# Moving the inverted 64-blocks of the second layer in transfers of sixteen partitions, from one spill tensor

## The chip, the cores and the metric

The kernel runs on one core of a Trainium2 chip. The metric is the time of one execution in device microseconds; the lower the better. TensorE (PE) does the matrix products, VectorE (DVE), ScalarE (ACT) and GpSimd (POOL) the elementwise work, and SyncE (SP) issues every DMA of this kernel, in the order of its program. An engine that waits holds up everything behind it in its own program.

## The reference, cut to what matters

The program is one step of a two-layer decoder for a prompt of 512 tokens and 8 samples. The change lies in the second layer, a gated DeltaNet with 16 query/key heads (the kernel calls each, with its two value heads, a pair) over 512 tokens. The prompt is cut into chunks; in each chunk and value head a unit lower triangular matrix is inverted and applied:

```
lmat = jnp.where(strict, jnp.einsum('bhnid,bhnjd->bhnij', kb, kc) * decay, 0.0)
tmat = lax.linalg.triangular_solve(lmat + eye, eye, left_side=True, lower=True, unit_diagonal=True)
u_val = tmat @ (vc * bc[..., None])
w_key = tmat @ (kb * jnp.exp(gc)[..., None])
...
v_new = u_n - w_n @ s
o_n = qd_n @ s + a_n @ v_new
s = s * gl_n[..., None, None] + jnp.swapaxes(kd_n, -1, -2) @ v_new
```

## The kernel before, in words

The weights are streamed: a half matrix of 512 KB (tile `wr`, three buffers) is loaded, split into a high part `wh` on ACT and a low part `wl` on DVE, and used by 48 matmuls of 260 columns into a `pg` tile. A `gemm` is two such halves.

Every call of an engine is recorded, and `flush` lays the instructions out with a planner: it keeps a clock for each engine, takes costs from the function `cost`, and writes each engine's instructions in the order of their planned start. For a DMA it plans an issue time on SP; a transfer over 20 KB that touches at most 8 partitions ("few", line 260) is planned at 1700 ns of SP, the others at 340 or 560 ns. Order is decided by these planned times; on the chip each engine follows the written order, whatever the times become. Each DMA also waits until the transfer eight issues before it has landed.

The second layer runs in two phases.

- **Phase one** (pool `l1a`). For each pair i, `prepare(i)` projects and convolves q and k (tiles `buf`, `cacc`, `kq`), forms the decay-weighted products and writes q, k, the product `it` and the lower triangular `lt` to `spill[i]` in DRAM: 4 chunks of 128 tokens x 128 partitions x 7 x 128 values, the slots 5 and 6 being `lt` of the two heads. After pair 15 come seven pairs of gate projections (`zd`, stored from tile `dd` with the DMA `z<-dd`).
- **Phase two** (pool `l1b`, which takes the memory of `l1a`). For each pair `values(i)` projects v (tiles `vc`, `vs`), `scan(i)` loads the four chunks of `spill[i]` (tile `pk`, four buffers) and runs the recurrence, `samples(i)` handles the 8 samples with the state tile `S`, and `normalise(i)` closes the pair.

`inverses(b8)` inverts the two 64x64 diagonal blocks of every chunk and head of eight pairs at once: 2 blocks x 8 pairs x 2 heads x 4 chunks are 128 matrices, one in each partition of tile `m` (128 x 64 x 64). It loads them from `spill`, works on DVE with some 120 products and reductions (`tmp<-m`, `m<-tmp`), and stores them back into `spill`. Loads and stores go block by block, pair by pair and head by head, four partitions each (one for each chunk): 32 transfers of 64 KB to load, 32 to store. Batch 0 (pairs 0 to 7) is recorded after pair 7 of phase one, with low urgency, batch 1 (pairs 8 to 15) in pieces over phase two (`background`). `scan(i)` needs the stores of its pair.

Of the kernel before, what the change touches and what calls it, by code (L numbers as in the profile page):

```python
# [8 lines left out]
F32 = mybir.dt.float32  # L9
# [6 lines left out]
P = 128  # L16
# [11 lines left out]
GQ = 16  # L28
# [10 lines left out]
class Sched:  # L39
# [79 lines left out]
    def region(self, ap):  # L119
        rec = self.owner.get(ap.tensor.name)  # L120
        if rec is None:
            return None
        dims, off = tuple(tuple(x) for x in ap.ap), ap.offset
        if ap.space == bass.MemoryType.DRAM:
            lo = off + sum(min(0, s * (c - 1)) for s, c in dims)
            hi = off + sum(max(0, s * (c - 1)) for s, c in dims)
            return rec, lo, hi + 1, 1
        if ap.space == bass.MemoryType.PSUM:
            return rec, 0, P, 1
        fs = 1  # L130
        for x in rec["shape"][1:]:
            fs *= x
        key = (off % fs, dims[1:])
        m = self.masks.get(key)
        if m is None:
            idx = np.array([off % fs])
            for s, c in dims[1:]:
                if s:
                    idx = (idx[:, None] + s * np.arange(c)[None, :]).reshape(-1)
            b = np.zeros(idx.max() + 1, np.uint8)  # L140
            b[idx] = 1
            m = self.masks[key] = int.from_bytes(np.packbits(b, bitorder="little").tobytes(), "little")
        p0 = off // fs
        return rec, p0, p0 + dims[0][1], m

    def record(self, eng, meth, fn, args, kw, out=None, ins=None, cost=None):
        isap = lambda x: isinstance(x, bass.AP)
# [81 lines left out]
    def cost(self, eng, meth, args, kw, out, ins):  # L229

        n = self.free(out)
        PSM = bass.MemoryType.PSUM
        big = [x for x in ins if not (self.free(x) == 1 and n > 1)]
        ptr = len(ins) - len(big)
        nps = sum(1 for x in ins if x.space == PSM)
        acc = kw.get("accum_out") is not None
        if eng == "PE":
            k, m = ins[0].shape[0], out.shape[0]
            rows = 32 if k <= 32 else 64 if k <= 64 else 128
            if meth == "transpose":  # L240
                return max(109 if rows == 128 else 82, 0.833 * n + 2), (rows, 128), "t"
            if ins[1].dtype == F32R:
                return (max(120, 0.417 * n + 6) if rows == 128 else 0.833 * n + 8), (rows, 128), "r"
            cols = 32 if m <= 32 else 64 if m <= 64 else 128
            if (rows, cols) == (128, 32):
                return max(100, 1.667 * n + 52), (rows, cols), "q"
            return 2 * max(109 if rows == 128 else 58, 0.833 * n + 3), (rows, cols), "f"
        if eng == "ACT":
            f = args[2] if meth == "activation" else AF.Copy
            return 0.83 * n + (58 if nps else 109) + 93 * ptr + 105 * acc, f  # L250
        if eng == "SP":
            by, run = int(4 * np.prod(out.shape)), 4096
            for x in [out] + ins:
                r = 1
                for st, c in reversed([tuple(d) for d in (x.ap if x.space == bass.MemoryType.DRAM else list(x.ap)[1:])]):
                    if st != r:
                        break
                    r *= c
                run = min(run, 4 * r)
            few = any(x.space != bass.MemoryType.DRAM and x.shape[0] <= 8 for x in [out] + ins) and by > 20000  # L260
            return (1700 if few else 340 if by / run <= 130 else 560), int(by * (1 + 77 / run if run >= 512 else 512 / max(run, 64)))
        two = sum(1 for x in big if x.space != PSM) > 1
        if eng == "DVE":
            fast = meth in ("tensor_scalar", "tensor_copy") and not nps and out.space != PSM
            if meth == "memset":
                return 0.52 * n + 60, True
            if meth == "reciprocal":
                return 6.6 * n + 70, False
            if meth == "tensor_tensor_scan":
                return 2.09 * n + 55, two  # L270
            if meth == "tensor_reduce":
                return 1.04 * self.free(ins[0]) + 65, False
            r = 0.52 if fast else 1.04
            if meth == "tensor_tensor" and n >= 100:
                inner = [[d for d in list(x.ap)[1:] if d[1] > 1] for x in big]
                if any(d and abs(d[-1][0]) > 4 for d in inner):
                    r = 1.83
            return r * n + 68 + 60 * ptr + 12 * acc, two or fast
        if meth == "tensor_tensor":
            return 1.57 * n + 430, True  # L280
        if meth == "tensor_reduce":
            return 2.1 * self.free(ins[0]) + 100, True
        if meth == "memset":
            return 0.5 * n + 130, True
        return 0.83 * n + 370 + 60 * ptr, True
# [198 lines left out]
def build(tc, a, ctx):  # L484
# [11 lines left out]
    dr = sc.pool(ctx, "dr", 1, DR)  # L496
# [610 lines left out]
    with ExitStack() as es:  # L1107
# [62 lines left out]
        for k in range(8):  # L1170
            for ip in range(len(X), max(k // 2 + 1, (k + 1) * KB // 8 // 2)):
                residual(ip)
            x = X[k // 2][:, k % 2]
# [46 lines left out]

    spill = [dr.tile([4, P, 7, P], F32, name=f"sp{i}") for i in range(GQ)]
    NZ = 7
    zd = [dr.tile([P, NT], F32, name=f"z{h}") for h in range(2 * GQ)]
    y1d = [dr.tile([P, NT], F32, name=f"y1_{h}") for h in range(NH)]
    with ExitStack() as l1:
# [124 lines left out]
        def inverses(b8, iv):  # L1352
            m = iv.tile([P, 64, 64], F32, name="m")
            blocks = []
            for blk in range(2):
                for i in range(8):
                    for hd in range(2):
                        p0 = blk * 64 + i * 8 + hd * 4
                        dv = spill[8 * b8 + i][:, blk * 64:blk * 64 + 64, 5 + hd, blk * 64:blk * 64 + 64]
                        blocks.append((m[p0:p0 + 4], dv))  # L1360
            for s, dv in blocks:
                Q.dma_start(s, dv)
            mf = m.rearrange("p j i -> p (j i)")
            V.memset(mf[:, 0::65], 1.0)
            pr = m[:, 32:64, 0:32]

            def dot(out, x, y):
                shape = x.shape[1:]
                n = int(np.prod(shape))
                tv = iv.tile([P, 1024], F32, name="tmp")[:, :n]  # L1370
                if len(shape) == 2:
                    tv = tv.rearrange("p (a b) -> p a b", a=shape[0])
                else:
                    tv = tv.rearrange("p (k a b) -> p k a b", k=shape[0], a=shape[1])
                V.tensor_tensor(tv, x, y, op=ALU.mult)
                V.tensor_reduce(out, tv, op=ALU.add, axis=AX.X)
                return n

            def diag(r0, nr, c0, nc_, step, nb):

                r = m[:, r0:r0 + nr, c0:c0 + nc_]
                return bass.AP(tensor=r.tensor, offset=r.offset, ap=[r.ap[0], [step * 65, nb], [64, nr], [1, nc_]])

            def over(x, n):

                return x.broadcast_to([P, x.shape[1], n, x.shape[3]])

            turn = lambda x: x.rearrange("p k a b -> p k b a")
            yield 0
            for i in range(1, 8):  # L1390
                x, col = diag(0, i, 0, i, 8, 8), diag(0, i, i, 1, 8, 8)
                yield dot(col[:, :, :, 0], x, over(turn(col), i))
            for s_ in (8, 16, 32):
                nb = 32 // s_
                prb = lambda j0, j1, k0, k1: bass.AP(tensor=pr.tensor, offset=pr.offset + 64 * j0 + k0,
                                                     ap=[pr.ap[0], [s_, nb], [64, j1 - j0], [1, k1 - k0]])
                for j in range(s_):
                    x = over(diag(j, 1, j, s_ - j, 2 * s_, nb), s_)
                    y = turn(diag(j, s_ - j, s_, s_, 2 * s_, nb))
                    yield dot(prb(j, j + 1, 0, s_)[:, :, 0, :], x, y)  # L1400
                for i in range(s_):
                    x = over(turn(diag(s_, i + 1, s_ + i, 1, 2 * s_, nb)), s_)
                    yield dot(diag(0, s_, s_ + i, 1, 2 * s_, nb)[:, :, :, 0], x, prb(0, s_, 0, i + 1))
            V.memset(pr, 0.0)
            for s, dv in blocks:
                Q.dma_start(dv, s)
# [69 lines left out]
        with ExitStack() as l1a:  # L1476
# [3 lines left out]
            for i in range(GQ):  # L1480
# [5 lines left out]
                if i in (1, 3, 5, 6)[:4 - 3]:  # L1486
                    ada(1, 8 + 3 + (1, 3, 5, 6).index(i), lk)
            back = [inverses(1, iv), 0]

            def background(n):  # L1490
# [273 lines left out]
        for i in range(GQ):  # L1764
# [4 lines left out]
            vs, dv = values(i)  # L1769
# [150 lines left out]
```

## Time and profile before

| | us |
|---|---|
| median of 3 runs | 3327.67 (3323.73 to 3341.83) |
| the profiled execution | 3313.89 |
| its span, first to last instruction | 3312.1 |
| PE busy in the span | 3108.7 (94%) |
| DVE busy | 2341.9 (71%) |
| ACT busy | 1566.5 (47%) |

Phase one of the second layer runs from about 1280 to 1870 us of the span, phase two to about 2920. A line of the trace gives the start, the duration, the engine, the operation, the tile written and the tiles read; what stands in brackets is the idle time of the engine before it, and what ended that. Since all instructions are laid out by one function, they carry the same line number (L418), and they are told apart by their tiles.

### The profile page before, as it was taken

The numbers are of one execution on the slowest core, as the hardware profiler recorded it, in microseconds if no ns is written. First come the engines' busy times: TensorE is split into PE (matmuls) and PEld (weight loads), VectorE is DVE, ScalarE is ACT, GpSimd is POOL, SyncE is SP. The second block draws the span as 40 slices with busy tenths as digits, with TensorE's granted clock in tenths as the row PEclk, the third lists the DMA queues.
The fourth block names the chain that finished last, engine by engine and source line by source line (L and its number), as shares of the span: only waits on it lengthen the run. The fifth ranks groups of instructions, "written<-read, shape, count | busy, mean of one in ns | idle before, by whom it ended". The sixth has DMA issues, their size and how long they took to land. (4 is left out here: it accounts for less than half of the span.)

```text
span 3312.1 us, 65624 instructions
## 1 busy us (share of the span) xinstructions
PE 3108.7 (94%) x24496; PEld 2806.7 (85%) x24496; DVE 2341.9 (71%) x6214; ACT 1566.5 (47%) x2927; POOL 342.6 (10%) x301
## 2 busy tenths in 40 slices
PE   8999999989979999999999668999989999999997
PEld 5898888877867777999999667987878989999997
DVE  3487989787864485668999426998975766566755
ACT  2234344434552366777652124545444655554544
POOL 0000000000001011111110011111112110101111
PEclk9999999999979999999999888998989999999999
DMA  9978989998538886776653255544446545376764
GB/s 317 298 256 290 316 299 315 304 319 305 175 119 282 296 294 210 162 163 151 146 151 116 74 113 145 140 141 145 139 126 186 149 145 161 119 231 211 225 185 139
DMA packets 361586, 667.02 MB, mean 201 GB/s; under 512 B 103697, under 2 KB 216338, under 8 KB 357170
## 3 DMA queue, kind: packets, MB, share of 16 engines
q1 hardware_dynamic: 361266, 662.82, 65.4%
q8 instruction: 193, 3.16, 0.4%
q14 instruction: 127, 1.04, 0.1%
HBM read 574.95 MB, written 87.70 MB: 200 GB/s over the span
## 5 line engine op out<-in xcount | busy, mean ns | idle before, releaser
L418 PE MATMUL pg<-uh,wh 128*128 128x260 f32 (+1 forms) x6112 | 1343.9, 289 | 6.6 <-ACT uh L418 3.1
L418 PE MATMUL pg<-ul,wh 128*128 128x260 f32 (+1 forms) x6112 | 1339.8, 289 | 1.5 <-DVE ul L418 1.1
L418 PEld LDWEIGHTS pg<-uh,wh 128*128 128x128 f32 (+1 forms) x6112 | 998.3, 190 | 62.2 <-issue 46.6
L418 PEld LDWEIGHTS pg<-ul,wh 128*128 128x128 f32 (+1 forms) x6112 | 998.9, 190 | 56.1 <-issue 43.6
L418 PE MATMUL pg<-uh,wl 128*128 128x260 f32 (+1 forms) x6112 | 892.0, 289 | 0.0
L418 DVE TENSOR_TENSOR wl<-wr,wh 128x1024 fp32r<-128x1024 f32 (+3 forms) x508 | 618.7, 1218 | 382.6 <-PE pg L418 161.5
L418 ACT CAST wh<-wr 128x1024 fp32r<-128x1024 f32 (+3 forms) x508 | 511.4, 1007 | 791.9 <-PE pg L418 671.3
L418 PEld LDWEIGHTS pg<-uh,wl 128*128 128x128 f32 (+1 forms) x6112 | 793.2, 190 | 46.6 <-issue 39.2
L418 DVE SCALAR_TENSOR_TENSOR junk<-page,qbc 128x128 f32<-128x128 f32 x1024 | 222.6, 284 | 9.7 <-ACT qbc L418 6.2
L418 DVE TENSOR_TENSOR tmp<-m 128x224 f32<-128x224 f32 (+19 forms) x238 | 214.5, 901 | 4.5
L418 DVE SCALAR_TENSOR_TENSOR acc<-gp,conv_w_a,acc 128x512 f32<-128x512 f32 x240 | 181.0, 754 | 6.6 <-ACT acc L418 3.9
L418 ACT ACT_TABLE_LOAD x120 | 154.0, 1283 | 49.8 <-DVE rs L418 19.5
L418 DVE TENSOR_REDUCE m<-tmp 128x32 f32<-128x224 f32 (+19 forms) x238 | 130.7, 549 | 3.3
L418 POOL TENSOR_SCALAR ctap<-buf,conv_w_c 128x512 f32<-128x512 f32 x64 | 72.7, 1135 | 524.9 <-ACT buf L418 521.5
L418 POOL TENSOR_TENSOR cacc<-cacc,ctap 128x512 f32<-128x512 f32 x64 | 84.9, 1326 | 388.6 <-DVE cacc L418 340.8
L418 DVE SCALAR_TENSOR_TENSOR cacc<-buf,conv_w_c,cacc 128x512 f32<-128x512 f32 x128 | 99.9, 781 | 13.9 <-ACT cacc L418 9.6
L418 PE MATMUL pl<-wa,cpad 128*32 128x512 f32 x512 | 81.0, 604 | 5.8 <-DMA wa<-w_ada 5.6
L418 DVE DVE_READ_ACCUMULATOR junk<-page,qbc 128x1 f32 x1024 | 81.4, 79 | 0.0
L418 PE MATMUL pg<-yh,wh 128*128 128x260 f32 x320 | 79.1, 283 | 0.0
L418 PE MATMUL pg<-yl,wh 128*128 128x260 f32 x320 | 78.9, 283 | 0.0
L418 POOL TENSOR_TENSOR S<-S,egb 128x2048 f32<-128x2048 f32 x16 | 59.5, 3722 | 165.4 <-PE pd L418 165.4
L418 PE MATMUL pl<-page,wst 128*32 128x512 f32 x512 | 75.1, 611 | 0.2
(377 smaller groups left out, 3615.5 us busy)
## 6 DMA issues: line engine op xcount, KB each, us to landing
wr<-w_in_odd SPq DMA_DIRECT2D x194, 512.0 KB
page<-cache_k SPq DMA_DIRECT2D x128, 512.0 KB
wa<-w_ada SPq DMA_DIRECT2D x128, 512.0 KB
page<-cache_v SPq DMA_DIRECT2D x128, 512.0 KB
wr<-w_out_odd SPq DMA_DIRECT2D x128, 512.0 KB
wr<-w_in_even SPq DMA_DIRECT2D x94, 512.0 KB
page<-w_ada SPq DMA_DIRECT2D x128, 256.0 KB
pk<-sp SPq DMA_DIRECT2D x64, 448.0 KB
```

What stands on the lines that cost most here:

```text
L418: o[2](*o[3], **o[4])
```

## The change

There is now one DRAM tensor `sp` for all pairs, 64 chunks x 128 x 7 x 128, of which `spill[i]` is a view. In `inverses` the partitions of `m` are dealt out anew: sixteen neighbouring partitions hold the four chunks of four neighbouring pairs for one block and one head, and they move in one transfer of 256 KB. There are 8 transfers instead of 32 to load a batch, and 8 instead of 32 to store it; the bytes and the length of the rows (64 values, 256 bytes) stay. The planner learns to tell the blocks of `sp` apart (`parts`), and prices transfers of up to 16 partitions as "few". What is computed is the same.

```
-            few = any(x.space != bass.MemoryType.DRAM and x.shape[0] <= 8 for x in [out] + ins) and by > 20000
+            few = any(x.space != bass.MemoryType.DRAM and x.shape[0] <= 16 for x in [out] + ins) and by > 20000
...
-    spill = [dr.tile([4, P, 7, P], F32, name=f"sp{i}") for i in range(GQ)]
+    spa = dr.tile([4 * GQ, P, 7, P], F32, name="sp")
+    spill = [spa[4 * i:4 * i + 4] for i in range(GQ)]
...
-            for blk in range(2):
-                for i in range(8):
+            for i in (0, 4):
+                for blk in range(2):
                     for hd in range(2):
-                        p0 = blk * 64 + i * 8 + hd * 4
-                        dv = spill[8 * b8 + i][:, blk * 64:blk * 64 + 64, 5 + hd, blk * 64:blk * 64 + 64]
-                        blocks.append((m[p0:p0 + 4], dv))
+                        p0 = 64 * blk + 32 * hd + 4 * i
+                        c0, r = 4 * (8 * b8 + i), slice(64 * blk, 64 * blk + 64)
+                        blocks.append((m[p0:p0 + 16], spa[c0:c0 + 16, r, 5 + hd, r]))
```

The planned order moves with it. On SP, at the end of phase one, the order before was this (the `z` stores are the last two gate stores, `wr` the weights of the second value head of pair 0):

```order
L418 DMA z_17871<-dd 128x520
L418 DMA wr<-w_in_odd 128x1024 x2
L418 DMA sp_17843<-m 4x64x64
...
L418 DMA sp_17850<-m 4x64x64
L418 DMA z_17872<-dd 128x520
L418 DMA sp_17850<-m 4x64x64
L418 DMA wr<-w_in_odd 128x1024
L418 DMA win<-state_conv_c 128x2x24
```

Now the same place reads:

```order
L431 DMA wr<-w_in_odd 128x1024 x2
L431 DMA sp<-m 16x64x64 x8
L431 DMA z_17856<-dd 128x520
L431 DMA z_17857<-dd 128x520
L431 DMA wr<-w_in_odd 128x1024 x3
L431 DMA win<-state_conv_c 128x2x24
L431 DMA zt<-z_17844 128x520
L431 DMA zt<-z_17845 128x520
L431 DMA pk<-sp 128x896 x3
```

Between the stores of the batch and the last gate store stood 31 transfers, now there are eight; but both last gate stores and the weights of pair 0's second value head now stand behind the stores, where one gate store and no such weight did.

On DVE, in phase one, the start of batch 0 (`MEMSET m`, which sets the diagonals) stood behind the work of pair 8:

```order
L418 SCALAR_TENSOR_TENSOR cacc<-buf,conv_w_c,cacc 128x512
L418 TENSOR_TENSOR wl<-wr,wh 128x1024
L418 TENSOR_TENSOR kql<-kq,kqh 128x1024
...
L418 TENSOR_TENSOR bet<-bet,ss 128x4x2
L418 MEMSET m 128x64
L418 TENSOR_SCALAR nb<-bet 128x8
```

Now it stands ahead of it:

```order
L431 SCALAR_TENSOR_TENSOR cacc<-buf,conv_w_c,cacc 128x512
L431 MEMSET m 128x64
L431 TENSOR_TENSOR tmp<-m 128x8
L431 TENSOR_REDUCE m<-tmp 128x8
L431 TENSOR_TENSOR tmp<-m 128x32
L431 TENSOR_TENSOR wl<-wr,wh 128x1024
```

Fifteen rows of pair 8 have moved behind the start of the batch. At the other end of the batch the closing `MEMSET m 128x32x32` stood behind the low part of the weights of pair 0's first value head; it now stands two such `wl` earlier, behind that of the last gate projection.

In phase two, on SP, the stores of batch 1 were spread over some fifty rows among weight loads. The new order is:

```order
L431 DMA S<-state_delta 128x2048
L431 DMA sp<-m 16x64x64
L431 DMA wr<-w_in_odd 128x1024
L431 DMA sp<-m 16x64x64 x6
L431 DMA zt<-z_17860 128x520
L431 DMA wr<-w_in_odd 128x1024
L431 DMA pk<-sp 128x896
L431 DMA sp<-m 16x64x64
L431 DMA pk<-sp 128x896
```

The first `pk` of pair 8 stands behind seven transfers of sixteen partitions, where it stood behind 20 of four.

## Rows read from the trace of the kernel before

**Rows 1.** Page: busy us of each engine; GB/s moved in 40 slices.

```profile
PE 3108.7 (94%) x24496; PEld 2806.7 (85%) x24496; DVE 2341.9 (71%) x6214; ACT 1566.5 (47%) x2927; POOL 342.6 (10%) x301
GB/s 317 298 256 290 316 299 315 304 319 305 175 119 282 296 294 210 162 163 151 146 151 116 74 113 145 140 141 145 139 126 186 149 145 161 119 231 211 225 185 139
```

**Rows 2.** Waits of PE, 1860 to 2550 us: total us, times, longest.

```profile
PE pm L418 <- ACT vc L418: 52.3, 1, 52.3
PE pm L418 <- DMA pk<-sp: 21.1, 4, 10.5
...
PE pd L418 <- DMA S<-state_delta: 5.5, 2, 5.0
```

**Rows 3.** Timeline of PE around its two longest waits: start us, us, instruction.

```profile
1869.84 2.09 PE L418 MATMUL pg<-uh,wl 128*128 128x260 f32 x16
1924.24 1.11 PE L418 MATMUL pm<-ct,vc 128*128 128x128 f32 x4 [52.31 <-ACT vc L418]
...
2485.21 0.39 PE L418 MATMUL pm<-ct,pk 64*64 64x64 f32 x2 [10.49 <-DMA pk<-sp]
```

**Rows 4.** Timeline of ACT over the change of phase.

```profile
1860.42 0.61 ACT L418 ACTIVATE dd<-pg 128x520 f32<-128x520 f32 x1 [0.88 <-PE pg L418]
1918.08 0.20 ACT L418 CAST selr<-ct 128x16 fp32r<-128x16 f32 x1 [57.05 <-DMA z<-dd]
```

**Rows 5.** Timeline of SP, DMA issues, 1850 to 2003 us.

```profile
1850.19 6.10 SPq L418 DMA_DIRECT2D wr<-w_in_odd  x2
1857.03 55.06 SPq L418 DMA_DIRECT2D sp<-m  x31
1912.19 1.56 SPq L418 DMA_DIRECT2D z<-dd  x1
...
2002.79 0.33 SPq L418 DMA_DIRECT2D m<-sp  x1
```

**Rows 6.** Busy us (instructions) in stretches; PEclk granted clock; DMA engines' share; GB/s.

```profile
1440.00:1520.00 80.00, 79.93 (x640) 77.02 (x639) 47.56 (x115) 60.88 (x89) 14.24 (x18) 1.00 0.72 161
...
1880.00:1900.00 20.00, 0.00 (x0) 0.00 (x0) 0.00 (x0) 0.00 (x0) 0.00 (x0) 0.50 0.22 37
...
1960.00:1980.00 20.00, 13.71 (x80) 12.66 (x79) 3.92 (x5) 3.13 (x6) 1.62 (x2) 0.74 0.49 118
...
2100.00:2400.00 300.00, 282.91 (x2202) 256.90 (x2201) 280.37 (x577) 152.05 (x403) 48.23 (x34) 0.95 0.49 144
2480.00:2500.00 20.00, 14.79 (x100) 12.78 (x100) 3.13 (x5) 5.22 (x15) 1.35 (x3) 0.74 0.65 201
```

**Rows 7.** DMA issues of one tile: ns min/median/max on SP.

```profile
L418 SPq DMA_DIRECT2D sp<-m x64: 266/1732/4675, 1857.0 to 2513.4; - x64
...
L418 SPq DMA_DIRECT2D o_cas<-win x8: 602/606/637, 194.4 to 878.3; - x8
```

**Rows 8.** Timeline of DVE at both ends of batch 0.

```profile
1506.96 0.74 DVE L418 SCALAR_TENSOR_TENSOR cacc<-buf,conv_w_c,cacc 128x512 f32<-128x512 f32 x1
...
1520.12 0.11 DVE L418 MEMSET m<- 128x64 f32 x1
...
1844.54 1.20 DVE L418 TENSOR_TENSOR wl<-wr,wh 128x1024 fp32r<-128x1024 f32 x1
...
1851.29 2.04 DVE L418 TENSOR_TENSOR tmp<-m 128x1024 f32<-128x1024 f32 x1
1853.36 1.22 DVE L418 TENSOR_REDUCE m<-tmp 128x32 f32<-128x1024 f32 x1
...
1856.10 0.91 DVE L418 MEMSET m<- 128x1024 f32 x1 [0.16 <-issue]
```

**Rows 9.** Timeline of SP around the stores of batch 1.

```profile
2423.86 3.19 SPq L418 DMA_DIRECT2D sp<-m  x3
...
2479.06 1.85 SPq L418 DMA_DIRECT2D pk<-sp  x2
...
2508.32 2.16 SPq L418 DMA_DIRECT2D S<-state_delta  x1
```

More of the change, by code (lines that the diff above doesn't have):

```diff
@@ L126, in region @@
             hi = off + sum(max(0, s * (c - 1)) for s, c in dims)
-            return rec, lo, hi + 1, 1
+            return rec, lo, hi + 1, self.parts(rec["shape"], dims, off) if len(rec["shape"]) == 4 else 1
         if ap.space == bass.MemoryType.PSUM:
@@ L144, in region, with parts @@
         return rec, p0, p0 + dims[0][1], m
+    def parts(self, shape, dims, off):
+        per = shape[1] * shape[2] * shape[3]
+        dims = tuple(d for d in dims if d[0] % per)
+        key = (off % per, dims, "parts")
+        if key not in self.masks:
+            idx = np.array([off % per])
+            for s, c in dims:
+                idx = (idx[:, None] + s * np.arange(c)[None, :]).reshape(-1)
+            p, s, f = np.unravel_index(idx, shape[1:])
+            self.masks[key] = sum(1 << int(q) for q in np.unique((p // 64 * shape[2] + s) * 2 + f // 64))
+        return self.masks[key]
     def record(self, eng, meth, fn, args, kw, out=None, ins=None, cost=None):
```

## The prediction, made before the changed kernel ran

> **What bounds the kernel now.** I read the page first. PE is busy for 94% of the span [rows 1], so only time in which PE stands still, or runs slowly after standing still, can be gained. The DMA throughput has a hole in the 23rd of 40 slices (74 GB/s, about 1820 to 1900 us), which is where the second layer goes from phase one to phase two. Next I asked who PE waits for between 1860 and 2550 us, since all transfers between `m` and `sp` but the first 32 loads lie there. One wait of 52.3 us stands out, then four for `pk` (21.1 us), then two for `S` (5.5 us) [rows 2]. Following the large one back: PE ends its last product at 1869.84 + 2.09 = 1871.9 and goes on at 1924.24, released by the tile `vc` [rows 3]. `vc` and all else of phase two lie in memory of phase one, and ACT's first instruction of phase two waits until 1918.08 for the last gate store `z<-dd` [rows 4]. Its data was there at 1860.42 + 0.61 = 1861.0. But SP issued it at 1912.19, behind 31 stores `sp<-m` that took SP from 1857.03 for 55.06 us [rows 5]. So the 52 us are the stores of batch 0: each holds SP for 55.06 / 31 = 1.78 us (the median of all 64 stores is 1.73 [rows 7]). While they run alone, DMA engines are busy for 0.22 of 16, that is 3.5 engines, at 37 GB/s [rows 6], and 65.5 KB in 1.78 us is 37 GB/s as well. Four engines work and twelve stand idle, as many as the transfer has partitions.
>
> **The change part by part.** The sum is made against the profiled execution (3313.9 us, with a span of 3312.1). The median of the runs shown lies 13.8 us above it, and I add those at the end.
>
> *Price of one transfer.* If the sixteen partitions occupy sixteen engines, each engine still gets 64 rows of 256 bytes, so a transfer takes 1.78 us and carries four times as much: eight take 14.2 us. SP needs about 0.6 us to issue one, by the row of `o_cas`, which also has 1024 runs [rows 7]. If they stay on four engines, or if 37 GB/s is what rows of 256 bytes allow in all, one takes 262 / 37 = 7.1 us and eight take 57 us. I take 1.78, since 3.5 busy engines at 37 GB/s look like engines at their limit, not like memory at its limit.
>
> The Trainium skill (DMA: Bandwidth & Descriptors, "Why a DMA increments its semaphore by 16 and not by 1") says that a transfer uses the largest number of engines, up to 16, that divides the slowest dimension of both sides. By it four partitions give four engines, as the 0.22 above shows, and sixteen give sixteen, which no run here shows yet; it raises the chance of the low price.
>
> The same page ("Anatomy of one DMA") gives, for the GpSimd path, 2.0 us plus the bytes at 436 GB/s for one transfer: 2.15 us for 64 KB against the 1.78 measured in a row of 31, and by estimate 2.6 us for 256 KB. By it the eight would take 20.8 us, and the sum would be some 6 us less good; the row is already below it, so I keep the row.
>
> *(A) The change of phase.* First, when does batch 0 end? Its last steps were a `wl` at 1844.54, the last product and reduction, one more `wl`, and the closing memset that ends at 1857.0 [rows 8]. In the new order that memset stands two `wl` earlier, directly behind the product and reduction that follow the `wl` of 1844.54: 1844.54 + 1.20 + 2.04 + 1.22 + 0.91 = 1849.9, if DVE keeps pace. DVE has the room: it drops two `wl` (2.4 us), and the batch starts behind the `cacc` of 1506.96, not at 1520.12 [rows 8], in 13 us in which DVE idles for about 40% (47.56 busy of 80 in the stretch before [rows 6]), so 5 us more. I take 1850 and keep 1857 as the late end. The eight stores then drain by 1850 + 0.6 + 14.2 = 1865. The last gate store has its data at 1861.0; it lands behind them at about 1867, and the weights of the second value head, issued behind it, need some 3 us to land and 1 us for `wh`: about 1871. PE ends the first value head at 1871.9. So the wait is 0 at 1850 and 5 to 6 us at 1857; I take 2. Gain 50, and 1 us more for the slow start: PE's granted clock was 0.50, 1.2 GHz, while it stood still [rows 6]. **A = -51** (from -53 to -42).
>
> What now stands behind the stores: both last gate stores and two weight halves. A half feeds PE for 48 matmuls, 48 x 79.93 / 640 = 6.0 us, and PE has the first value head (12 us) in hand. That covers the 14 us if the batch ends by 1852 or so; past that each us costs one.
>
> *(B) Loads of batch 1.* The 32 loads were issued among weights and `pk` until 2002.79 [rows 5]. Of the four waits for `pk` (21.1), 10.5 belong to C, so 10.6 are here [rows 2]. In 1960 to 1980 PE had a granted clock of 0.74 and took 13.71 us for 80 matmuls, which take 10.0 us at 0.125 each (640 in 79.93), so 3.7 more are lost [rows 6]. In the new order three of pair 0's four `pk` stand ahead of all loads, and the loads take 14 us of DMA instead of 57. From 14.3 I take **B = -10** (from -14 to -5): pair 0's recurrence has short waits of its own that move with it.
>
> *(C) Stores of batch 1.* They began at 2423.86, the first `pk` of pair 8 followed at 2479.06, and `S` at 2508.32 [rows 9]. PE waited 10.5 us for that `pk` [rows 3] and 5.0 for `S` [rows 2], and ran at 0.74 afterwards: 14.79 us for 100 matmuls instead of 12.5 [rows 6]. Together 17.8. Now the `pk` stands behind seven stores, 12 us. The planner also asks for it earlier, so some wait stays: **C = -14** (from -18 to -8).
>
> *(D) DVE.* Batch 1 starts earlier against PE's work, because its loads end earlier. From 2100 to 2400 DVE is busy for 280.4 of 300 us and PE loses 17.1 [rows 6]. With the same DVE work spread wider, part of this returns: **D = -5** (from -20 to +5).
>
> *(E) First loads of batch 0 and the rest.* PE is busy for 79.93 of 80 us there [rows 6]; nothing can be gained. `MEMSET m` now stands in front of pair 8's work on DVE and waits for the last four loads; four loads are 7 us, behind a store that must land. What is late there is covered by the weight halves in hand. For this and for new small waits in the new order I add **E = +4** (0 to +8). The finer bookkeeping of blocks, the new view and the prices in the planner cost nothing at run time; they act through the order alone.
>
> Sum: -51 - 10 - 14 - 5 + 4 = -76. 3313.9 - 76 = 3237.9, and with the 13.8 to the median **3252**. All good ends (-105) give 3223, all poor ends (-42 - 5 - 8 + 5 + 8 = -42) 3286.
>
> **The rivals.**
> *The gain is partly taken back by DVE.* Batch 1 now runs beside pair 0's recurrence, whose steps go back and forth between PE, ACT and DVE. If 1925 to 2040 then runs like 2100 to 2400, where 2202 matmuls (275 us at 0.125) took 300, it loses 8%, 10 us, B and D are gone and A and C come out at their poor ends: -42 - 8 + 10 = -40, time 3288. For it: DVE's 93% there. Against: before, DVE stood nearly idle in 1960 to 1980 (3.92 of 20 us), and the work fits.
> *The sixteen partitions do not spread, or do not run faster.* Then one transfer takes 7.1 us. At the change of phase eight take 57 us as before, with two weight halves behind them: about 1850 + 57 + 6 = 1913 against 1924.24, -11. In phase one DVE stands at `MEMSET m` for four loads, 28 us less the 7 planned, which PE's two halves in hand (12 us) cover in part: +9, and the same for batch 1: +9. At the stores of batch 1 seven stand in a row, 50 us with one weight half among them; three halves in hand cover 18, so 32 stand where 17.8 stood: +14. Together +21, time 3349, **slower**. It decides from about 6 us a transfer, on the line between -76 at 1.78 us and +21 at 7.1. Against it: the 3.5 busy engines.
> *More returns than I count.* If DVE's wait in 2100 to 2400 goes altogether and the batch ends by 1850, the sum is near -105: 3223.
>
> **How the numbers follow.** Forecast 0.70, DVE rival 0.17, no spreading 0.07, more 0.06. A difference of 0.5% (16.6 us) is about what a measurement of this kernel can tell from none. Faster by more than that, below 3311: all of forecast, DVE rival and more, less 0.02 for a poor order: 0.91. Slower, above 3344: 0.04. Within: 0.05. The range goes from the good ends, 3223, to past the DVE rival, 3300; what is left out is the case without spreading and a little on both sides.
>
> **What would show it.** (A) PE's wait for `vc` at the change of phase under 8 us, the eight stores issued within 15 us, 0.8 or more of the DMA engines busy while they run. (B) No wait of PE for `pk` over 3 us before pair 1. (C) The wait at pair 8 under 5 us. (D) PE above 95% where batch 1 runs. Wrong would be: stores that hold SP for 5 us or more each; a closing memset of batch 0 later than 1857; or a new wait of PE for DVE in pair 0 of over 10 us.

## The result, and the profile after

The changed kernel takes 3247.2 us (median of 4, 3244.6 to 3250.0) where the kernel before takes 3325.7 beside it: a ratio of 0.975, 95% interval 0.972 to 0.979. That is 78 us or 2.4% faster; 3252 was forecast, inside the range. The profiled execution took 3244.6 us, with a span of 3242.8.

The page of the changed kernel, busy time of each engine and GB/s in 40 slices. [rows 1] holds the same lines of before:

```profile
PE 3094.5 (95%) x24496; PEld 2791.6 (86%) x24496; DVE 2344.5 (72%) x6214; ACT 1570.1 (48%) x2928; POOL 345.4 (11%) x301
...
GB/s 312 295 276 292 304 314 301 319 307 313 203 94 263 290 312 252 139 161 154 149 149 131 110 158 144 143 151 141 142 200 129 171 124 156 137 247 199 227 182 137
```

PE has the same 24496 instructions. Its span less its busy time fell from 203.4 to 148.3 us, so 55 of the 69 us are standing still that went away. The other 14 are in the busy time itself: the same matmuls ran for less time at the low clock (mean granted clock 0.963 before, 0.973 after). The hole in the 23rd slice is filled from 74 to 110 GB/s, though the slice is not quite the same stretch: it lies from 1784 to 1865 us now, and the stores of batch 0 reach into the next one.

Who PE waited for, from 1280 to 2500 us (total us, times, longest), against [rows 2]:

```profile
PE pm L431 <- DVE vdh L431: 14.8, 2, 13.8
PE pg L431 <- ACT wh L431: 10.6, 1, 10.6
PE pm L431 <- DVE kql L431: 7.9, 1, 7.9
...
PE pd L431 <- DVE qs L431: 4.4, 1, 4.4
PE pd L431 <- DMA S<-state_delta: 3.9, 1, 3.9
```

The 52.3 us for `vc` became 10.6 us for a weight half, and the 21.1 us for `pk` are gone. But two waits are new: 7.9 us for `kql` (the low part of `kq`) and 13.8 us for `vdh` (made from `vn` and the decay in the recurrence), both on DVE.

SP around the change of phase (start us, us, instruction), against [rows 5]:

```profile
1857.83 20.37 SPq L431 DMA_DIRECT2D sp<-m  x8
1878.30 5.01 SPq L431 DMA_DIRECT2D z<-dd  x2
1883.40 0.98 SPq L431 DMA_DIRECT2D wr<-w_in_odd  x2
```

Eight stores hold SP for 20.37 us, 2.55 each, where 31 held it for 55.06. The two stores of gates and the weights still queue behind them. PE's last work before its wait, and ACT's cast of the weight half that ends the wait:

```profile
1877.96 2.09 PE L431 MATMUL pg<-uh,wl 128*128 128x260 f32 x16
1889.54 1.05 ACT L431 CAST wh<-wr 128x1024 fp32r<-128x1024 f32 x1 [3.23 <-DMA wr<-w_in_odd]
```

DVE at both ends of batch 0, at the first step of phase two, and PE where its three largest waits end:

```profile
1515.88 0.11 DVE L431 MEMSET m<- 128x64 f32 x1 [9.65 <-DMA m<-sp]
...
1856.89 0.91 DVE L431 MEMSET m<- 128x1024 f32 x1 [0.16 <-issue]
1886.01 0.10 DVE L431 MEMSET oss<- 128x10 f32 x2 [16.19 <-DMA z<-dd]
```

```profile
1519.69 0.58 PE L431 MATMUL pm<-kql,kqh 128*128 128x256 f32 x1 [7.89 <-DVE kql L431]
...
1890.63 0.80 PE L431 MATMUL pg<-uh,wh 128*128 128x260 f32 x2 [10.59 <-ACT wh L431]
1940.35 0.55 PE L431 MATMUL pm<-vdh,th 128*128 128x256 f32 x1 [13.77 <-DVE vdh L431]
```

`MEMSET m` opens a batch and needs all of its loads. In batch 0 the last four were issued from 1497.65 to 1502.84 and the memset ran at 1515.88; the split of `kq` stands behind it on DVE, and PE waited for that.

Where the gain lies is read between marks that both programs have: PE's return after the change of phase (1924.24 in [rows 3], 1890.63 above; it has done 14268 matmuls by then in both), and its product of `S` and `es`, which it runs once per pair, at pairs 1, 7 and 9. Windows of PE between these marks, before and after (length, busy time of PE, PEld, DVE, ACT and POOL with instructions, PE's granted clock, share of the DMA engines, GB/s):

```profile
0.00:1924.24 1924.24, 1808.09 (x14268) 1591.50 (x14269) 1374.36 (x4317) 875.53 (x1338) 139.57 (x157) 0.97 0.74 231
1924.24:2061.04 136.80, 118.52 (x827) 108.71 (x827) 67.21 (x160) 47.56 (x109) 14.45 (x14) 0.85 0.56 139
2061.04:2422.78 361.74, 338.86 (x2618) 307.23 (x2617) 339.27 (x699) 184.51 (x488) 55.56 (x39) 0.93 0.49 142
2422.78:2562.26 139.48, 123.99 (x977) 113.49 (x975) 80.72 (x182) 66.08 (x173) 22.60 (x20) 0.94 0.58 160
```

```profile
0.00:1890.63 1890.63, 1810.31 (x14268) 1590.60 (x14268) 1374.55 (x4315) 876.39 (x1336) 143.24 (x155) 0.98 0.77 235
1890.63:2002.06 111.43, 97.65 (x755) 89.89 (x755) 70.67 (x165) 44.94 (x107) 13.29 (x13) 0.91 0.79 163
2002.06:2367.20 365.14, 344.44 (x2695) 313.80 (x2693) 342.00 (x699) 189.02 (x491) 56.11 (x42) 0.94 0.49 142
2367.20:2491.09 123.89, 118.23 (x917) 107.13 (x916) 72.32 (x176) 63.93 (x170) 19.48 (x17) 0.94 0.65 175
```

The order moves some matmuls over a mark, so each stretch is put right by 0.125 us a matmul, the 79.93 us for 640 of [rows 6]. Up to pair 1, for instance, after needs 136.80 - 111.43 = 25.4 us less for 72 matmuls less, so 25.4 - 9.0 = 16.4 are gained. For after, and for four of the kernels below, the us against before:

| kernel | to PE's return | to pair 1 | pairs 1 to 7 | pairs 7 to 9 | the rest | sum |
|---|---|---|---|---|---|---|
| after | -33.6 | -16.4 | -6.2 | -8.1 | -4.9 | -69.3 |
| e_store4 (only loads changed) | -1.8 | -20.4 | -20.0 | +21.7 | +19.7 | -1.0 |
| e_load4 (only stores changed) | -21.6 with the next | | -0.6 | -11.8 | +15.3 | -18.7 |
| e_price_b | -63.0 with the next | | -18.8 | -19.1 | +11.2 | -89.7 |
| e_store32 | -66.6 with the next | | -19.9 | -18.3 | 0.0 | -104.9 |

The four were run on other chips, where before itself was 8 to 12 us faster by the medians; the table is for where the time lies, and the ratios below for how much it is.

### The profile page after: what moved, and what is told of

Its sections match the earlier page's. It is cut to its first block, busy times and chain, and to the rows that moved or that the text cites. A ratio compares the mean times of both kernels' runs of the same rounds, so it can differ in the third digit from the quotient of the medians.

```text
span 3242.8 us, 65556 instructions
## 1 busy us (share of the span) xinstructions
PE 3094.5 (95%) x24496; PEld 2791.6 (86%) x24496; DVE 2344.5 (72%) x6214; ACT 1570.1 (48%) x2928; POOL 345.4 (11%) x301
## 5 line engine op out<-in xcount | busy, mean ns | idle before, releaser
L431 POOL TENSOR_TENSOR cacc<-cacc,ctap 128x512 f32<-128x512 f32 x64 | 89.7, 1402 | 363.9 <-DVE cacc L431 253.5
L431 DVE DVE_READ_ACCUMULATOR junk<-page,qbc 128x1 f32 x1024 | 91.2, 89 | 0.0
```

Source lines behind the costliest of these rows:

```text
L431: o[2](*o[3], **o[4])
```

## The experiments

The theory: transfers of sixteen partitions free SP's queue, and that is the gain; what is still lost are loads that land later than the planner thinks and stores that cost 2.55 us. The rivals: the gain comes from the loads alone, from the stores alone, or from the order that the cheaper price gives the planner. A fourth was not run: the new tensor and the new dealing of the partitions, with transfers of four both ways, so what these two bring by themselves is not shown. The kernel before took 3314 to 3318 us in these comparisons, so kernels are compared by their ratio to it:

| kernel | ratio to before | 95% interval |
|---|---|---|
| after, run again (e_after) | 0.976 | 0.975 to 0.978 |
| e_store4 | 0.999 | 0.997 to 1.000 |
| e_load4 | 0.994 | 0.992 to 0.996 |
| e_eight | 0.987 | 0.985 to 0.988 |
| e_twice | 0.985 | 0.982 to 0.987 |
| e_store32 | 0.968 | 0.967 to 0.970 |
| e_price / e_price_b | 0.972 / 0.973 | 0.970 to 0.975 / 0.971 to 0.975 |
| e_price70 | 0.987 | 0.985 to 0.989 |
| e_nz8 | 0.983 | 0.981 to 0.986 |
| e_both | 0.979 | 0.976 to 0.981 |
| e_z3 | 0.971 | 0.969 to 0.973 |

### Loads or stores (e_after, e_store4, e_load4)

> The changed kernel once more, unaltered, so that the three kernels beside it and the one with the dearer price have a run of it to stand against: 0.975 of the kernel before, with the three waits of TensorE at 7.9, 10.6 and 13.8 us again.

```
 stores of e_store4 (the loads of e_load4 in the same way):
             for s, dv in blocks:
-                Q.dma_start(dv, s)
+                for j in range(0, 16, 4):
+                    Q.dma_start(dv[j:j + 4], s[j:j + 4])
```

> The changed kernel with its loads as they are, but the stores of both batches in transfers of four partitions again (32 instead of 8 in a batch). Theory (the stores of batch 0 stand between VectorE's last step and the loads behind them): 32 stores of 1.78 us are 57 us in place of 20.4, so TensorE's wait at the change of phase is 10.6 + 36.6 = 47 us, and the wait for pk at pair 8 comes back with some 10 us; with the lower clock that follows a long wait 40 to 60 us more than the changed kernel. Rival (the gain comes from the loads or from the planner's order): 0 to 15 us more.

> The changed kernel with its stores as they are, but the loads of both batches in transfers of four partitions again (32 instead of 8 in a batch). Theory (each transfer of four partitions holds the queue about 1.8 us, so 57 us for the loads of batch 1 ahead of those of pk): the gain at the change of phase stays (wait of 8 to 12 us), the two waits for pk of 10.5 us come back in pair 0, the wait of 13.8 us for vdh goes or stays: 5 to 25 us more than the changed kernel. Rival (the loads bring the gain, through an earlier start of VectorE on batch 0): the wait at the change of phase grows by over 20 us and most of the gain is lost, 40 us or more over the changed kernel.

The changed kernel came out as before, with waits of 7.1, 8.8 and 12.7 us at the three places. Measured in one comparison: after 3237.5, e_store4 3311.7 (74 us more, over the 40 to 60 expected), e_load4 3295.3 (58 more, over the 5 to 25). Before was 3317.8. So the new loads alone save 6 us, which the interval of the ratio hardly tells from none, the new stores alone 22, both 80. SP in e_store4, and its PE where the largest wait ends:

```profile
1853.21 57.36 SPq L431 DMA_DIRECT2D sp<-m  x32
```

```profile
1922.47 1.11 PE L431 MATMUL pm<-ct,vc 128*128 128x128 f32 x4 [47.07 <-ACT vc L431]
```

The 47 us are as expected, so the stores are what PE waits for at the change of phase. The table of stretches shows why the parts don't add. Up to pair 1 they nearly do: 22.2 by the loads, 21.6 by the stores, 50.0 by both. Later they don't. By pair 7 the loads alone are 42 us ahead, and they lose 41 from there on. Half of that lies from pair 7 to 9, where the 32 small stores of batch 1 are issued: PE waits 18.7 us for `pk` and 7.2 for `S`, and its granted clock is 0.86 where it was 0.94:

```profile
2382.75:2556.67 173.92, 144.32 (x1079) 131.78 (x1077) 92.99 (x194) 70.31 (x177) 23.15 (x21) 0.86 0.51 134
```

There, what came early to a full queue waited longer in it. The other half lies behind pair 9, where no wait is over 2.2 us and the granted clock was 0.82 from 2606 to 2709.5 us; no run tells what makes it. In e_load4 the gaps of the loads stay: 12.8 us for `kql`, since the memset of batch 0 waited 14.8 us for its last loads, and 13.9 for `pk` in pair 0. PE's waits in e_load4, 1280 to 2000 us:

```profile
PE pm L431 <- DMA pk<-sp: 13.9, 2, 9.0
PE pm L431 <- DVE kql L431: 12.8, 1, 12.8
PE pg L431 <- ACT wh L431: 9.1, 1, 9.1
```

Neither text of e_load4 fits as a whole: the time is as large as its rival had it, but the wait at the change of phase stayed at 9.1 us as its theory had it. Of the 51 us by which it falls short of after in the table, 28 lie up to pair 1 and 20 behind pair 9, where no wait is over 3.2 us; why these 20 are lost stays open.

### What a transfer costs (e_eight, e_twice, e_store32)

> The changed kernel with transfers of eight partitions, sixteen loads and sixteen stores in a batch. Theory one (a transfer costs by its rows, 1024 rows in 2.55 us, so 512 in 1.3): the stores of batch 0 hold the queue 20 to 22 us as now, 0 to 4 us more than the changed kernel. Theory two (a transfer costs by the rows of one partition, 64 rows in 1.78 us however many partitions go beside it, up to the engines): 16 x 1.78 = 28.5 us, so the wait at the change of phase is 8 us longer, and the loads of batch 1 are longer as well, 8 to 18 us more than the changed kernel.

> The eight stores of batch 0 are issued twice, so sixteen transfers stand behind the closing memset, and nothing else changes. Theory (each store holds the queue 2.55 us, all of it in TensorE's way at the change of phase): 20 us more wait there, 10.6 to 31, span 3260 to 3266, median 3264 to 3270. Rival one (a store holds the queue only 0.4 us and the wait is the time to landing): 3 us more, median 3248 to 3253. Rival two (the second eight go at the 1.78 us that the prediction took): 14 us more, median 3259 to 3263.

> The changed kernel with its loads as they are and the stores in transfers of 32 partitions, four in a batch, of 512 KB each. Measured so far for one store in a row of them: 1.79 us of the queue with 4 partitions, 1.88 with 8, 2.55 with 16. Theory one (from 16 partitions on a transfer costs by its rows, 2.5 ns each): 5.1 us each, 20.4 us for the four, the change of phase as in the changed kernel, 0.975 to 0.978 of before. Theory two (the price goes on growing more slowly than the rows): 3.5 to 4 us each, 14 to 16 us, the wait at the change of phase 4 to 6 us shorter, 0.972 to 0.975.

```
 e_twice:
-            for s, dv in blocks:
+            for s, dv in blocks + blocks * (1 - b8):
                 Q.dma_start(dv, s)
 e_store32:
-            for s, dv in blocks:
-                Q.dma_start(dv, s)
+            for blk in range(2):
+                for hd in range(2):
+                    p0, r = 64 * blk + 32 * hd, slice(64 * blk, 64 * blk + 64)
+                    Q.dma_start(spa[32 * b8:32 * b8 + 32, r, 5 + hd, r], m[p0:p0 + 32])
```

Windows inside the row of batch 0's stores in e_store4, e_eight, e_twice and e_store32, one fence each. The last columns are PE's granted clock, the busy share of the 16 DMA engines and GB/s:

```profile
1858.00:1908.00 50.00, 17.39 (x145) 17.19 (x143) 2.45 (x2) 1.66 (x2) 0.00 (x0) 0.70 0.21 36
```

```profile
1862.00:1888.00 26.00, 17.69 (x148) 17.48 (x146) 2.45 (x2) 1.66 (x2) 0.00 (x0) 0.92 0.42 68
```

```profile
1860.00:1895.00 35.00, 19.08 (x159) 18.87 (x157) 2.45 (x2) 2.58 (x3) 0.00 (x0) 0.83 0.74 97
```

```profile
1858.00:1868.00 10.00, 10.00 (x86) 10.00 (x85) 1.49 (x2) 2.10 (x2) 0.00 (x0) 1.00 0.90 159
```

And the stores on SP, in e_eight, e_twice and e_store32:

```profile
1860.02 30.12 SPq L431 DMA_DIRECT2D sp<-m  x16
```

```profile
1856.42 40.10 SPq L431 DMA_DIRECT2D sp<-m  x16
```

```profile
1857.21 9.51 SPq L431 DMA_DIRECT2D sp<-m  x4
```

From 4 to 8 partitions the engines' share and the rate double and a transfer costs the same, 1.79 and 1.88 us. From 8 to 16 the share grows by only 1.8 and the rate by 1.4, and a transfer costs 2.5. From 16 to 32 the rate grows by 1.6 again: 512 KB at 159 GB/s are 3.3 us. Neither theory of e_eight fits the whole ladder; theory two of it holds up to 8, theory two of e_store32 beyond (3.5 to 4 expected, 3.3 found).

Divided by the engines that are busy, the ladder shows more. The shares are 3.4, 6.7, 11.8 and 14.4 busy engines of 16 for 4, 8, 16 and 32 partitions, so a busy engine moved 10.7, 10.1, 8.2 and 11.0 GB/s, or took 24, 25, 31 and 23 ns for a piece of 256 bytes. With 4 and 8 partitions an engine has 64 pieces to move, 1.5 to 1.6 us of the price; with 32 it has 128 if two partitions go to each, by that estimate 3.0 of the 3.3 us. So in these three the price is mostly the pieces of one engine at one speed, as the prediction had it, and sixteen partitions are the exception: their pieces take a third longer, and a quarter of the engines' time is idle. That so many engines are at work cannot be the reason, since more are with 32. What the reason is was not tried.

The Trainium skill (DMA: Bandwidth & Descriptors, "Anatomy of one DMA") gives, for the GpSimd path, 2.0 us plus bytes at 436 GB/s; by that estimate 2.6 and 3.2 us for 16 and 32 partitions, near the 2.55 and 3.3 here on SP's queue, while 4 and 8 partitions are cheaper than its 2.15 and 2.3.

e_twice puts the price on PE's path: eight more stores make its wait for `vc` 31.9 us where the one stall at the change of phase was 10.6, that is 2.66 us for each, and cost 27 us in all by the ratios, 7 more than expected (8.6 us for `pk` came along). PE's wait in e_twice:

```profile
PE pm L431 <- ACT vc L431: 31.9, 1, 31.9
```

e_eight lost 35 us, far over its 8 to 18: the longer stores are 22.6 us of wait for `vc` there, and 12.7 for `pk` and 15.2 for `y` followed that neither theory had.

e_store32 is the best kernel of all: 3.2% under before, 0.8% under after, below what either of its theories gave. It has no wait over 1.2 us at the change of phase (1840 to 1921), and `vdh` fell to 1.7 although its DVE waited 18.3 us at the memset of batch 1, which the planner, with another price for the larger stores, had placed elsewhere. What is left is a wait for `S` behind the loads (8.9 us), and the 7.4 us for `kql`, since its loads have the old price. So the size of a transfer and the order changed together in this run, and how much each brought isn't told apart.

### The planner's price (e_price, e_price_b, e_price70)

```
-            return (1700 if few else 340 if by / run <= 130 else 560), int(by * (1 + 77 / run if run >= 512 else 512 / max(run, 64)))
+            return (1700, int(by * 3.3)) if few and by == 262144 else ((1700 if few else 340 if by / run <= 130 else 560), int(by * (1 + 77 / run if run >= 512 else 512 / max(run, 64))))
```

e_price70 has `(6800, int(by * 1.5))` in that place.

> Only the planner's price of a sixteen-partition transfer changes: 262144 x 3.3 / 335 = 2.6 us of transfer each in place of 1.6, near the 2.55 us at which the eight stores of batch 0 left the queue in the changed kernel. The transfers are the same; in VectorE's order the closing memset of the diagonal of batch 0 now stands behind the split of kq that TensorE waits for, not ahead of it. Theory (the memset stands ahead of work that TensorE needs, and the loads are later than the planner thinks): the 7.9 us wait of TensorE for kql at 1520 goes, the 13.8 us wait for vdh at 1940 shrinks to under 5, the wait at the change of phase stays at 8 to 14 us; 10 to 19 us less, a span of 3224 to 3233, a median of 3228 to 3237. Rival (VectorE has no room, so a later start only moves the wait to the end of the batch): the two waits go, but the wait at the change of phase grows by as much; 3242 to 3252.

> The kernel with the dearer price (2.6 us of transfer) once more, so that it and the two kernels with another order beside it stand against the same runs: 0.972 of the kernel before, with one wait of TensorE left at the change of phase, for vc, of 12 to 16 us, and none over 3 us for kql or vdh.

> The changed kernel's transfers, but planned as if each cost what four transfers of four partitions cost before: 6.8 us of the queue and 1.2 us of bytes. The planner then orders the rest much as it did for the 32 transfers. Theory (the gain comes from the shorter transfers, the order of the rest matters by 10 to 20 us): 0.970 to 0.980 of before, the two waits for kql and vdh gone, some wait for pk in pair 0 or at pair 8 instead, since loads and stores are planned late. Rival (the gain comes from the order that the cheaper price allows, not from the transfers): most of the gain is lost, 0.990 to 1.000.

e_price measured 0.972 and, run again, 0.973: some 12 us under the changed kernel by the ratios, as the theory had it. The intervals of the repeats just touch (0.971 to 0.975 against 0.975 to 0.978). PE's waits in e_price, 1280 to 2500 us:

```profile
PE pm L431 <- ACT vc L431: 14.8, 1, 14.8
PE pl L431 <- DVE oss L431: 5.5, 3, 2.3
PE pm L431 <- ACT sth L431: 1.7, 1, 1.7
```

Neither `kql` nor `vdh` is left; the memset now stands behind the split of `kq` in DVE's order and waits for no load. The wait at the change of phase grew by 4 us. So these two waits of the changed kernel were a matter of order, made by a planner that took a transfer to be done earlier than it is.

e_price70 shows that the order can also take much back: 0.987, outside both expectations, about half of the gain lost. It keeps up until pair 7 (2345.9 against 2343.1 in e_price_b), and loses from 2440 us on, with its window first and that of e_price_b behind it:

```profile
2440.00:2680.00 240.00, 213.12 (x1500) 185.45 (x1501) 149.39 (x371) 126.05 (x355) 34.53 (x30) 0.86 0.48 140
```

```profile
2440.00:2680.00 240.00, 231.04 (x1775) 204.48 (x1774) 160.18 (x389) 136.29 (x373) 33.98 (x28) 0.95 0.50 151
```

PE gets 1500 matmuls done instead of 1775, with many waits of under 4 us and at a granted clock of 0.86 instead of 0.95. Which step of the order makes these wasn't tried. So the rival of the order is half right: the transfers open the gain, and the price that the planner puts on them decides how much of it is collected.

### The change of phase (e_nz8, e_both, e_z3)

```
 e_nz8, e_both:
-    NZ = 7
+    NZ = 8
 e_z3 (with the price of e_price):
-            for s, dv in blocks:
+            for s, dv in blocks[:8 if b8 else 3]:
                 Q.dma_start(dv, s)
+            if not b8:
+                rest.extend(blocks[3:])
...
+            sc.later = len(sc.ops) - 1
+            with sc.prio(3000):
+                for s, dv in rest:
+                    Q.dma_start(dv, s)
```

> Eight pairs of gates instead of seven are multiplied in phase one (NZ = 8): two gemms more, some 23 us of TensorE work, stand before the change of phase, and are gone from pair 7 of phase two. Theory (the 10.6 us wait of TensorE at 1880 to 1890 is only the time that the eight stores and the transfers behind them need after VectorE's last step): that wait falls under 2 us, the others stay (7.9 and 13.8), 8 to 11 us less: span 3232 to 3235, median 3236 to 3239. Rival (pair 7 of phase two, paced by VectorE, loses the gemms that fill TensorE's gaps there): the wait goes and as much comes back in phase two, 3244 to 3252.

> The price of e_price and the eighth gate pair of e_nz8 together. Theory (three separate waits of 7.9, 10.6 and 13.8 us, all of them the price of late loads and stores): the gains add, 18 to 30 us less than the changed kernel, a median of 3217 to 3229, with no wait of TensorE over 5 us from 1490 to 2000. Rival (VectorE is the bound there): one of the two gains only, 3232 to 3240.

> The kernel with the dearer price, and the last store of gates put ahead of the last five of the eight stores of batch 0 in the DMA queue. With the dearer price alone that gate was ready at 1856.3, was issued at 1868.4 behind five stores, and landed at 1875.8; VectorE's first step of phase two waited 18.9 us for it and TensorE 14.8 us behind that. Theory (the wait at the change of phase is the queue position of that one transfer): it is issued near 1858 and lands 8 to 10 us earlier, the wait falls from 14.8 to 3 to 7 us, 7 to 12 us less than the kernel with the dearer price alone, near 0.969 of before. Rival (the stores hold back the weights and pk of pair 0 in any case): the wait moves to a weight half or to pk, and the time stays within 4 us of the kernel with the dearer price.

Two more gate products in phase one did cover the wait there: e_both has no wait over 5 us from 1840 to 1960, and from 1840 to 1900 PE is busy throughout. Yet both kernels got slower: e_nz8 by 23 us against after (0.983), e_both by 21 against e_price. Windows of e_both and of e_price_b:

```profile
2425.00:2800.00 375.00, 354.44 (x2629) 311.97 (x2627) 238.35 (x586) 200.83 (x549) 53.48 (x41) 0.90 0.48 143
```

```profile
2425.00:2800.00 375.00, 366.04 (x2882) 329.30 (x2881) 244.87 (x601) 210.99 (x570) 55.84 (x44) 0.97 0.50 150
```

In the pairs from 8 on PE stands still for 20.6 us instead of 9.0 and its clock is granted at 0.90 instead of 0.97. That fits the rival of e_nz8, that phase two needs these products to fill PE's gaps, at a higher price than written; that it is these products that are missing there was not tried by itself. In e_nz8 the wait for `vdh` did not stay either: one of 14.3 us for `S` stands in its place.

In e_z3 five of the stores wait for the last gate to be issued. The gate moved as planned (SP, then PE's waits):

```profile
1857.61 0.34 SPq L431 DMA_DIRECT2D z<-dd  x1
1857.99 12.24 SPq L431 DMA_DIRECT2D sp<-m  x5
1870.33 6.33 SPq L431 DMA_DIRECT2D wr<-w_in_odd  x2
```

```profile
1873.83 1.12 PE L431 MATMUL pm<-ct,vc 128*128 128x128 f32 x4 [5.34 <-ACT vc L431]
1899.22 0.66 PE L431 MATMUL pm<-ct,vc 128*128 128x128 f32 x4 [4.45 <-ACT vc L431]
1932.15 0.80 PE L431 MATMUL pm<-sth,th 128*128 128x256 f32 x2 [6.11 <-ACT sth L431]
```

DVE enters phase two at 1863.28 instead of 1882.08. The one wait of 14.0 us fell apart into 5.3, 4.5 and 6.1, and the ratio, 0.971 against 0.973, is no different within the intervals. The rival fits best: the weights stand behind the stores in any case, and the wait moved. The medians are 6 us apart, though, which is over the 4 that it allowed and short of the theory's 7 to 12.

## Why the prediction was right, point by point

**Price of a transfer.** The step that was mis-sized is "each engine still gets 64 rows of 256 bytes, so a transfer takes 1.78 us". A store takes 2.55, the share of busy DMA engines was 0.70 to 0.74 and not 0.8, and the eight took 20.4 us, not 15. The rows do spread over the engines (11.8 are busy by the 0.74 in e_twice), but a busy one moved 8.2 GB/s, where it had moved 10.5 before (37 GB/s by 3.5 engines). Why it is slower with sixteen partitions, and not with 32, stays open. The sentence beside it, 2.6 us by the Trainium skill's formula (DMA: Bandwidth & Descriptors, "Anatomy of one DMA"), was the better price, and the sum it gave, 6 us less good, was nearer. That this sum came within a microsecond is partly chance: the price explains about 6 of the 13 us by which A and E fell short, and B made up for the others.

**(A) and (E), change of phase and first loads.** Forecast -47 together, at the poor end -34; it was -33.6. The wait for `vc` of 52.3 became one of 10.6 where I had 2, with 5 to 6 as the poor end. From the end of the batch to PE's return I had about 21 us, from 1850 to 1871; it took 32.8, from 1857.8 to 1890.6. Of these 11.8 us, about 6 are the stores (20.4 for 14.2). The rest is what stands behind them: two gate stores held SP for 5.0 us more, where I had 2 for the last one to land, and the weight half took 6.1 us from its issue at 1883.40 to its cast at 1889.54, where I had 3 that no row shows.

The batch itself ended at 1857.8, where I had 1850 and had called anything later than 1857 a sign of error. The step "DVE has the room" failed: the batch began at 1515.9 and not at 1507, and took 341.9 us from its first memset to the end of its last, where it had taken 336.9. This did not lengthen the wait, since PE came 8.1 us late as well (1880.0 for 1871.9), nearly all of it its new wait of 7.9 us at 1520. Both the late start and that wait come from E: I gave the last four loads 7 us and trusted to the weights in hand, and they landed 13 us after the last was issued. e_price shows that the 7.9 was a matter of order. So the 13.4 us by which A and E fell short are 8.6 of the wait and, of PE's 8.1 us delay, the 4 that E did not cover, to within a microsecond.

**(B) Loads of batch 1.** Forecast -10, -14 at best; it was -16.4. No wait for `pk` is left, as forecast, but the sign of error that I had named came as well, a wait for DVE in pair 0 of over 10 us: 13.8, since `MEMSET m` stood ahead of `vdh` in DVE's order and waited for loads issued until 1923. That the stretch gained more all the same says that the queue had cost more than its waits for `pk`: all of pair 0 ran at a clock of 0.85 before and of 0.91 after. PE stood still for 18.3 us before and for 13.8 after, which is 4.5 of the 16.4; the other 11.9 are matmuls that ran nearer to 0.125 us each. e_store4, with the new loads and the old stores, confirms the size: -20.4.

**(C) Stores of batch 1.** Forecast -14; -8.1 up to pair 9 and -4.9 behind it, which I put here though no run shows that they belong here. PE no longer waits for `pk`, and 3.9 us for `S`.

```profile
2368.64 16.24 SPq L431 DMA_DIRECT2D sp<-m  x6
2384.93 3.62 SPq L431 DMA_DIRECT2D zt<-z  x1
2388.66 1.26 SPq L431 DMA_DIRECT2D wr<-w_in_odd  x1
2390.09 1.06 SPq L431 DMA_DIRECT2D pk<-sp  x1
```

The `pk` of pair 8 still queues behind the stores, 23 us instead of the 55 of [rows 9], and now PE has work in hand for that long.

**(D) DVE.** Forecast -5, it was -6.2. But PE did not get above 95% where batch 1 runs by much: 286.95 of 300 us in 2040 to 2340, 95.6%, against 94.3% in the same stretch of the work in [rows 6].

```profile
2040.00:2340.00 300.00, 286.95 (x2267) 262.05 (x2265) 282.54 (x576) 155.42 (x403) 46.45 (x34) 0.95 0.50 145
```

The rival that DVE takes the gain back was right in its place only, with the 13.8 us in pair 0.

**The sum.** -69.3 against -76: short by 13.4 in A and E, ahead by 6.4 in B, the rest within 1.3. The profiled execution came out 6.7 us over its sum, and the median 4.8 under its forecast, since the 13.8 us that I added for the distance between the two shrank to 2.6. The closeness of the median is owed to that.

## What to carry to other kernels

Ask of every transfer in a row how many DMA engines it keeps busy: a queue with engines idle gives its time back to whoever waits behind it once more partitions go into one transfer, and here it went on to 32. When a transfer gets cheaper, measure it and put the new price into whatever orders the work, since an order made for a wrong price took back some 12 us here and 47 in the worst trial (e_price70 against e_price_b). Price loads by when the last one lands, not by what the queue needs to issue them, and look at the next place where the same queue is full before counting a gain twice.

## What the runs showed of the hardware that was not expected

- The price of a row of stores of 256-byte pieces grows slowly with the partitions in each: 1.79, 1.88 and 2.55 us on the queue for 4, 8 and 16, and 3.3 us by the rate for 32, at 36, 68, 97 and 159 GB/s. A busy engine moved 10.7, 10.1, 8.2 and 11.0 GB/s: sixteen partitions are the slow case, and 32 are not.
- Loads of the same shape were issued by twos and fours, so none stood in a long row; the median issue took SP 0.43 us and the longest 3.87, but the last four of batch 0 landed 13 us after the last issue, beside weights and other stores.
- TensorE's busy time for the same 24496 instructions went from 3108.7 us before to 3094.5 after and 3085.8 in e_store32, and up to 3117.3 in e_nz8, with mean granted clocks of 0.963, 0.973, 0.980 and 0.966. Waits cost more than their length: in pair 0 before, PE took 13.71 us for 80 matmuls around its wait for `pk`, at a clock of 0.74 [rows 6], which take 10.0 at full clock. The mean clock alone does not order the busy time, since before has its lowest clock, 0.50, where PE stood still for 52 us.
